# Fixing ScalarE's order around the token-major projections, folding a sigmoid into an eviction, and moving convolution taps to the sample part

## The chip, the cores and the metric

The kernel runs on one core of a Trainium2 chip. The metric is the time of one execution on the device, in microseconds. Beside that time the profile gives the span of one profiled execution, and the two are kept apart below.

## What is computed

One inference step of a decoder trunk with two layers. In each layer the rows of a prompt (16 learned tokens and 1024 new ones) and of 64 sample tokens (8 sequences of 8) are normalised and projected, and three mixers work on the projections: a gated linear recurrence, a depthwise convolution behind a gated linear unit (GLU), and sparse attention whose keys an indexer chooses. Their outputs are gated, merged, projected and added to the stream. Cut to what the change touches:

```python
def project(h, norm_g, w_in, b_in):
    u = rmsnorm(h, norm_g) @ w_in + b_in

def conformer_conv(glu_in, z, buf, conv_w, conv_b, ln_g, ln_b, conv_pw, w_pb):
    a, g = jnp.split(glu_in, 2, axis=-1)
    u = a * jax.nn.sigmoid(g)
    xp = jnp.concatenate([buf.astype(u.dtype), u], axis=1)
    y = lax.conv_general_dilated(xp, conv_w...) + conv_b       # 31 taps per channel, 512 channels

def index_scores(qi, wi, ki):
    s = jnp.einsum('bqhd,bsd->bqhs', qi.astype(F32), ki.astype(F32))
    return jnp.einsum('bqhs,bqh->bqs', jax.nn.relu(s), wi.astype(F32) * IDX_SCALE)
```

The keys of the indexer (`ki`), its queries (`qi`), the attention's keys and values pass through a rotation (rope) first. The scores of the prompt are computed against the 1040 prompt keys, those of the sample tokens against the cached pages and the 64 new keys; the best 256 keys of each query are then selected.

## The kernel before

Activations stand feature-major: 128 features on the partitions, 1104 tokens along the free axis, split into a high and a low part (`XH`, `XL`), and each weight likewise (`wh`, `wl`), so that a product takes three matmuls on TensorE (PE).

**Feature-major projections.** `stream` (L342 to L406) walks over chunks of 128 output features. A chunk has three token groups (384, 384 and 336 wide), each a chain of 24 matmuls into one PSUM bank, and ScalarE (ACT) evicts each group with its bias through the helper `act_` (L204), to a buffer `sp` that goes to DRAM after the third (L404): `gaD` and `ggD` are the value and the gate of the GLU, four chunks each. ACT casts the high part of the next weights (`wh<-wr`, L269), and GpSimd (POOL) subtracts for the low part (`wl`, L270). The stream is a generator: other stages call `fill(key)`, which issues so many matmuls' worth of it by a table.

**Token-major projections.** `cproj` (L658 to L693) computes what is needed token by token: keys, values, indexer queries and keys. Two groups of 290 columns, each nine token tiles of 24 matmuls (L679 to L681) into the banks that `stream` uses too (five banks in all); ACT evicts each tile to `CTr` (L684), POOL adds the bias (L685), and for the second column group VectorE (DVE) applies the rope (L718 to L722).

**Index keys and scores.** `indexer` (L725 on) casts the index keys (`rl<-CTr`, ACT L733), subtracts for the low part (POOL L734), transposes on PE (L739) and evicts to `KIH` and `KIL` (ACT L743, L744). Between these steps `fill` issues stream matmuls. L777 is the first PE step behind the last cast of a key. Then, for each tile of 128 queries and each of four heads, PE writes scores to one buffer of two banks (`lg`, L770, L771), ACT applies the relu (`rl<-lg`, L204) and DVE accumulates (L803, L805): the score loop. The sample part follows: POOL gathers pages of cached keys (`kir`, L880), PE transposes them (L888), ACT casts them, PE multiplies, and DVE builds the score rows in two rounds (L831, L833, L834); L869 writes the score bank anew.

**The taps.** `conv` (L1462 to L1503) has four chunks of 31 taps. A tap is two DVE operations, `cy<-up` on 128x1040 (L1495) and `cy<-us` on 128x64 (L1496); the first of a chunk is L1492 and L1493. `gated(c)`, called in the middle of the chunk before, loads the value into `up` and the gate into `cy` (L1473), applies the sigmoid in place on ACT (L1476), and multiplies on POOL (L1477, L1478, behind a memset L1470 and a copy L1475). `up` and `cy` have two buffers, so chunk 2 waits for chunk 0's last tap. Each tap costs 1420 units of a budget that the table `SIDE` gives to stages; a stage issues taps until its debt is paid: `t0` beside the feature-major chunks, `tr` (one value per token tile) behind each rope, `tk` behind the index keys, `ti` in the score loop, `ts` (twice per layer, once in each round) in the sample part. `SIDE` thus sets how many of a layer's 124 taps stand where in DVE's order.

**What sets the order.** PE's instructions stand in text order throughout, and DVE's from the attention stage on. Those of ACT, POOL and SyncE (SP) are placed by the scheduler of the framework, which estimates when each can start; on the chip every engine runs its list strictly in that order, and an instruction whose input is late holds up all behind it.

Of the kernel before, what the change touches and what calls it, by code (L numbers as in the profile page):

```python
# [11 lines left out]
def _quiet(msg, *args, **kwargs):  # L12
# [10 lines left out]
AF = mybir.ActivationFunctionType  # L23
# [26 lines left out]
SIDE = {"t0": (5000, 10000, 10000, 10000, 9300, 10000), "tr": (4200, 4200, 4200, 4200, 4200, 4200, 4200, 2000, 0),  # L50
# [3 lines left out]
KSEL = 4  # L54
# [100 lines left out]
def trunk(tc, a, o, depth=DEPTH):  # L155
# [47 lines left out]
    def act_(out, in_, fn, **kw):  # L203
        S.activation(out, in_, fn, **kw)  # L204
# [136 lines left out]
    def stream(l, pv, chunks, groups, slot, early, lead, more):  # L341


        n = len(chunks)
        blocks = chunks + [("early", (c, bi)) for c in range(8) for bi in range(2)]
        parts = [(c, g) for g in range(3) for c in range(lead)]
        parts += [(i, g) for i in range(lead, n - 2) for g in range(3)]
        parts += [(i, g) for g in range(3) for i in (n - 2, n - 1)]
        parts += [(i, g) for i in range(n, n + 16) for g in range(3)]
        ws, bufs = {}, {}  # L350

        def get(i):
            if i < len(blocks) and i not in ws:
                nm, c = blocks[i]
                if nm == "early":
                    ws[i] = ws[i - 2][1:] if c[0] % 2 else wpair(l, BLK["pb" if c[1] else "pa"] + c[0] // 2)
                else:
                    ws[i] = wchunk(l, BLK[nm] + c, V if i == lead else G, more if 1 < i < lead else None)

        get(0)  # L360
        get(1)
        yield True
        for i, g in parts:
            if g == 0 and 0 < i < lead - 1:
                get(i + 1)
            if lead <= i < n - 1 or i >= n or (i in (lead - 1, n - 1) and g == 2):
                get(i + 1)
            nm, c = blocks[i]
            if nm == "early":
                yield from early.part(c[1], c[0], g, ws[i][0], slot[0])  # L370
                continue
            bcol = BCOL[nm]
            wh, wl = ws[i]
            if g == 0:
                bufs[i] = spt(more if 1 < i < lead else None)
            n0, nn = groups(nm)[g]
            ps = slot[0]()[:, 0:nn]
            sl = slice(n0, n0 + nn)
            H, L = ([x[:, k, sl] for k in range(8)] for x in (XH, XL))
            if i == 0:  # L380

                ops = []
                for k in range(10):
                    if k < 8:
                        ops += [(wh(k), H[k]), (wl(k), H[k])]
                    if k > 1:
                        ops.append((wh(k - 2), L[k - 2]))
            else:
                ops = [(wh(k), x[k]) for k in range(8) for x in (H, L)] + [(wl(k), H[k]) for k in range(8)]
            for j, (w, x) in enumerate(ops):  # L390
                T.matmul(ps, w, x, start=(j == 0), stop=(j == 23))  # L391
                if j == 23:

                    fn = AF.Sigmoid if nm == "gate" and c < 16 else AF.Identity
                    act_(bufs[i][:, sl], ps, fn, bias=pv[:, bcol + c:bcol + c + 1])
                    if nm in ("cz",):

                        if g == 0:
                            sg = spt()
                        act_(sg[:, sl], ps, AF.Sigmoid, bias=pv[:, bcol + c:bcol + c + 1])  # L400
                        G.tensor_tensor(bufs[i][:, sl], bufs[i][:, sl], sg[:, sl], op=OP.mult)
                    if g == 2:
                        lo = groups(nm)[0][0]
                        S.dma_start(fD[nm][c, :, lo:NT], bufs[i][:, lo:NT])  # L404
                    if i == n - 1:
                        early.load(g)  # L406
                if j % 3 == 2:
                    yield True
# [164 lines left out]
    def layer(l, hst, late):  # L573
# [39 lines left out]
        slot[0] = mmt  # L613
        ctp = ctr.enter_context(tc.tile_pool(name="ctr", bufs=1, side="right"))
        CTr = ctp.tile([128, 9, 580], F32, name="CTr", tag="CTr")
        cproj(l, CTr, taps)
        scp = scs.enter_context(tc.tile_pool(name="scp", bufs=1))
        SC = scp.tile([128, SCN], F32, name="SC", tag="SC")
        SC8 = scp.tile([128, NT], F32, name="SC8", tag="SC8")
        fill("ic")  # L620
        indexer(l, CTr, SC, SC8, fill, taps)
        ctr.close()
        tk1 = tks.enter_context(tc.tile_pool(name="tk1", bufs=1))
        steps, F = topk(SC, SC8, tk1)
# [30 lines left out]
        return merge(l, pv, late_groups, fill, ers)  # L655


    def cproj(l, CTr, taps):  # L658
        with tc.tile_pool(name="cpk", bufs=CPK, side="right") as cpk, tc.tile_pool(name="cpr", bufs=2, side="right") as cpr, \
                tc.tile_pool(name="cpt", bufs=2, side="right") as cpt:  # L660
            for gi, (c0, w) in enumerate(CGROUPS):
                brep = cpr.tile([128, 290], F32, name="brep", tag="brep")
                Y.dma_start(brep[:, 0:w], a["b_in"][l, c0:c0 + w].partition_broadcast(128))
                ch, cl = [], []
                for k2 in range(4):
                    cr = cpr.tile([128, 2, 290], F32, name="cr", tag="cr")
                    Y.dma_start(cr[:, :, 0:w], a["wc"][l, gi, k2])
                    for k in range(2):
                        h_ = cpk.tile([128, 290], F32R, name="ch", tag="ch")
                        l_ = cpk.tile([128, 290], F32R, name="cl", tag="cl")  # L670
                        S.copy(h_[:, 0:w], cr[:, k, 0:w])
                        G.tensor_tensor(l_[:, 0:w], cr[:, k, 0:w], f(h_[:, 0:w]), op=OP.subtract)
                        ch.append(h_)
                        cl.append(l_)
                for t in range(9):
                    rows, ts = TROWS[t], slice(128 * t, 128 * t + TROWS[t])
                    ps = dmt()
                    for k in range(8):
                        T.matmul(ps[0:rows, 0:w], XH[:, k, ts], ch[k][:, 0:w], start=(k == 0), stop=False)  # L679
                        T.matmul(ps[0:rows, 0:w], XH[:, k, ts], cl[k][:, 0:w], start=False, stop=False)  # L680
                        T.matmul(ps[0:rows, 0:w], XL[:, k, ts], ch[k][:, 0:w], start=False, stop=(k == 7))  # L681
                    d0 = c0 - O_C - 512
                    dst = CTr[0:rows, t, d0:d0 + w]
                    S.copy(dst, ps[0:rows, 0:w])  # L684
                    G.tensor_tensor(dst, dst, brep[0:rows, 0:w], op=OP.add)  # L685
                    if gi == 1:
                        rope(CTr[0:rows, t, 0:576].rearrange("p (h d) -> p h d", d=64), 9, t, rows, cpt, ((0, 2), (4, 9)))
                        taps("tr", t)
            for dst, j0, j1 in ((kvD.rearrange("t p c -> (t p) c"), 0, 256), (o["kv"][l], 0, 256), (o["ki"][l], 512, 576)):
                Y.dma_start(dst[0:1024].rearrange("(t p) c -> p t c", p=128), CTr[:, 0:8, j0:j1])  # L690
                Y.dma_start(dst[1024:NT], CTr[0:80, 8, j0:j1])
# [30 lines left out]
            V.tensor_tensor(x[:, h0:h1, 0:16], A[0:rows, h0:h1], B[0:rows, h0:h1], op=OP.add)  # L722


    def indexer(l, CTr, SC, SC8, fill, taps):  # L725
        with tc.tile_pool(name="ixc", bufs=1) as xc, tc.tile_pool(name="ixt", bufs=2) as xt:
            KIH = xc.tile([128, NT], F32R, name="KIH", tag="KIH")
            KIL = xc.tile([128, NT], F32R, name="KIL", tag="KIL")
# [6 lines left out]
            for t0 in range(0, 9, 4):  # L735
                n = min(4, 9 - t0)
                ps, w = tpt(), 0
                for t in range(t0, t0 + n):
                    T.transpose(ps[:, w:w + TROWS[t]], kk[0:TROWS[t], t], ident[0:TROWS[t], 0:TROWS[t]])  # L739
                    w += TROWS[t]  # L740
                sl = slice(128 * t0, 128 * t0 + w)
                for e in (slice(0, 64), slice(64, 128)):
                    S.copy(KIH[e, sl], ps[0:64, 0:w])  # L743
                    S.copy(KIL[e, sl], ps[64:128, 0:w])  # L744
                if t0 == 8:
                    V.tensor_tensor(ki8, f(KIH[0:64, sl]), f(KIL[0:64, sl]), op=OP.add)
                fill("ik", t0 // 4)

            wsc = xc.tile([128, 9, 4], F32, name="wsc", tag="wsc")
            V.tensor_scalar(wsc[:, 0:8], CTr[:, 0:8, 576:580], 0.0625, None, op0=OP.mult)  # L750
# [713 lines left out]
    def conv(l, pv, cw, c1):  # L1464
        def gated(c):
# [7 lines left out]
            Y.dma_start(y, fD["gg"][c])  # L1473
            Y.dma_start(sr[:, 0], a["state_conv"][l, c])
            G.tensor_copy(us[:, :, 0:30], sr[:, 0])  # L1475
            act_(y, y, AF.Sigmoid)  # L1476
            G.tensor_tensor(up[:, 30:1070], up[:, 30:1070], y[:, 0:1040], op=OP.mult)  # L1477
            G.tensor_tensor(us[:, :, 30:38], us[:, :, 30:38], y[:, 1040:1104].rearrange("p (b q) -> p b q", q=8), op=OP.mult)  # L1478

# [6 lines left out]
        for c in range(4):  # L1486
            up, us, y = nxt
# [288 lines left out]
```

## Time and profile before

| | |
|---|---|
| median of 3 runs | 2927.29 us (2923.65 to 2928.7) |
| profiled execution, time | 2926.8 us |
| profiled execution, span | 2924.9 us |
| mean granted clock of TensorE | 0.979 |
| busy: PE, DVE, ACT, POOL | 94%, 72%, 41%, 43% of the span |

The span covers the first to the last instruction; 1.9 us lie around it. A row of a timeline gives the start, the duration and, in brackets, how long the engine had idled and what ended the wait. Time is saved where PE idles, since it is busy for 94% of the span; idle time of the other engines matters where PE waits for them. The two layers run the same program; layer 0's stage of interest lies at 100 to 460 us, layer 1's at 1540 to 1860 us.

### The profile page before, as it was taken

How to read it: one execution, taken by the hardware profiler on the slowest of the kernel's cores; microseconds unless marked ns; L12 is line 12 of the kernel's file. 1: busy time of each engine (PE TensorE's matmuls, PEld its weight loads, DVE VectorE, ACT ScalarE, POOL GpSimd, SP SyncE). 2: the span in 40 equal slices, each digit the busy share in tenths (PEclk: the TensorE clock that was granted, in tenths of full speed). 3: DMA queues.
4: the chain of work that ended last, by engine and by line, in shares of the span. 5: the costliest groups of instructions: out<-in, count | busy, mean ns of one | idle time of the engine just before them, and what ended most of it. 6: DMA issues, size and time to landing. Idle time of an engine off the chain costs nothing. (4 is left out here: it accounts for less than half of the span.)

```text
span 2924.9 us, 44993 instructions
## 1 busy us (share of the span) xinstructions
PE 2757.9 (94%) x17094; PEld 2620.9 (90%) x17094; DVE 2113.7 (72%) x3832; ACT 1186.8 (41%) x2369; POOL 1247.6 (43%) x978
## 2 busy tenths in 40 slices
PE   7989899999998999999999998998999999999898
PEld 7988879999998888879999997898999989988798
DVE  5798867889969667535366896788899786774443
ACT  4314443323333556544341334422332335565432
POOL 3533334434425214756564332443434241157563
PEclk9999999999999999999999999999999999999999
DMA  4523234332335124666453322323332441247554
GB/s 146 162 61 109 90 103 140 122 112 89 118 130 170 67 67 154 195 201 197 150 169 105 98 83 90 127 99 109 130 112 77 157 151 63 86 150 222 190 166 148
DMA packets 192569, 374.14 MB, mean 128 GB/s; under 512 B 30657, under 2 KB 129697, under 8 KB 192289
## 3 DMA queue, kind: packets, MB, share of 16 engines
q1 hardware_dynamic: 166016, 272.21, 29.7%
q10 hardware_dynamic: 20448, 78.09, 6.6%
q0 software_dynamic: 5888, 20.97, 2.3%
q8 instruction: 134, 2.20, 0.3%
q14 instruction: 83, 0.67, 0.1%
HBM read 251.07 MB, written 122.40 MB: 128 GB/s over the span
## 5 line engine op out<-in xcount | busy, mean ns | idle before, releaser
L391 PE MATMUL mm<-xh,wh 128*128 128x384 f32 (+2 forms) x2656 | 888.1, 336 | 27.6 <-ACT sp L204 23.9
L391 PE MATMUL mm<-xl,wh 128*128 128x384 f32 (+2 forms) x2656 | 886.0, 336 | 0.0
L270 POOL TENSOR_TENSOR wl<-wr,wh 128x512 fp32r<-128x512 f32 x332 | 473.1, 1443 | 697.8 <-ACT wh L269 465.8
L391 PEld LDWEIGHTS mm<-xh,wh 128*128 128x128 f32 x2656 | 506.0, 191 | 41.5 <-ACT sp L204 29.0
L391 PE MATMUL mm<-xh,wl 128*128 128x384 f32 (+2 forms) x2656 | 531.3, 336 | 0.0
L391 PEld LDWEIGHTS mm<-xl,wh 128*128 128x128 f32 x2656 | 506.2, 191 | 7.2 <-issue 1.9
L391 PEld LDWEIGHTS mm<-xh,wl 128*128 128x128 f32 x2656 | 461.8, 192 | 6.3 <-issue 1.9
L916 DVE TENSOR_SCALAR_CACHE_REDUCE jk<-SC,F 80x1104 bf16<-80x1104 f32 (+6 forms) x448 | 448.8, 1002 | 8.4
L204 ACT ACTIVATE sp<-mm,vec 128x384 f32<-128x384 f32 (+1 forms) x356 | 198.6, 564 | 512.0 <-PE mm L391 494.8
L1495 DVE SCALAR_TENSOR_TENSOR cy<-up,vec,cy 128x1040 f32<-128x1040 f32 x240 | 337.9, 1408 | 0.4
L269 ACT CAST wh<-wr 128x512 fp32r<-128x512 f32 x352 | 203.6, 618 | 164.1 <-PE mm L391 80.4
L204 ACT ACTIVATE P<-P,nm 128x896 f32<-128x896 f32 (+7 forms) x128 | 99.5, 778 | 64.1 <-DVE nm L1021 61.7
L1037 DVE TENSOR_TENSOR pl<-tp,ph 128x512 fp32r<-128x512 f32 x144 | 97.8, 687 | 36.9 <-ACT ph L1036 36.1
L1496 DVE SCALAR_TENSOR_TENSOR cy<-us,vec,cy 128x64 f32<-128x64 f32 x240 | 117.2, 488 | 0.0
L1036 ACT CAST ph<-tp 128x512 fp32r<-128x512 f32 x144 | 83.2, 584 | 54.4 <-PE tp L1033 50.2
L1021 DVE CUSTOM_DVE_ANT_0 P<-sc,MB 128x512 f32<-128x512 f32 (+1 forms) x96 | 63.9, 667 | 57.1 <-PE sc L1015 56.2
L1346 PEld LDWEIGHTS lg<-hQ,hK 128*128 128x128 f32 x512 | 65.8, 205 | 28.0 <-issue 19.9
L1025 DVE TENSOR_SCALAR P<-P,nm 128x896 f32<-128x896 f32 (+7 forms) x128 | 87.4, 683 | 4.3
L1346 PE MATMUL lg<-hQ,hK 128*128 128x64 f32 x512 | 66.4, 286 | 25.5 <-DVE hQ L1375 25.3
L1033 PE MATMUL tp<-ident,P 128*128 128x128 f32 x576 | 88.0, 275 | 1.5 <-DVE P L1025 1.5
L204 ACT ACTIVATE rl<-lg 128x1024 f32<-128x1024 f32 (+6 forms) x54 | 42.6, 788 | 102.8 <-DVE SC L805 60.2
L287 PE MATMUL tp<-xh,wh 128*128 128x384 f32 (+2 forms) x240 | 79.9, 335 | 0.4 <-DVE z L1681 0.4
(454 smaller groups left out, 5932.0 us busy)
## 6 DMA issues: line engine op xcount, KB each, us to landing
wr<-in_wp SPq DMA_DIRECT2D x180, 512.0 KB
eg<-gateD SPq DMA_DIRECT2D x80, 184.0 KB
gateD<-sp ACTq DMA_DIRECT2D x24, 552.0 KB
gateD<-sp ACTq DMA_DIRECT2D x24, 544.0 KB
cr<-in_wc SPq DMA_DIRECT2D x16, 290.0 KB
gt<-gateD SPq DMA_DIRECT2D x24, 192.0 KB
za<-zaD SPq DMA_DIRECT2D x24, 192.0 KB
ggD<-sp ACTq DMA_DIRECT2D x8, 552.0 KB
```

The costliest lines, as they stand in the source:

```text
L204: S.activation(out, in_, fn, **kw)
L269: S.copy(wh[:, k:k + 4], wr[:, k:k + 4])
L270: (eng or G).tensor_tensor(wl[:, k:k + 4], wr[:, k:k + 4], f(wh[:, k:k + 4]), op=OP.subtract)
L391: T.matmul(ps, w, x, start=(j == 0), stop=(j == 23))
L916: V.tensor_scalar(jk[0:rows, 0:n], s, F.bitcast(F32)[0:rows, j:j + 1], None, op0=OP.is_ge, op1=OP.add, accum_out=cnt[0:rows, j:j + 1])
L1025: V.tensor_scalar(p[:, 0:n], p[:, 0:n], nm[:, 3:4], None, op0=OP.mult)
L1033: T.transpose(ps[:, 128 * c:128 * c + 128], P[c][:, 128 * kt:128 * kt + 128], ident)
L1036: S.copy(ph, ps)
L1037: V.tensor_tensor(pl, ps, f(ph), op=OP.subtract)
L1346: T.matmul(ps[:, 64 * c:64 * c + 64], K[:, 128 * c:128 * c + 128], up(Q[:, 128 * c:128 * c + 128], m), start=True, stop=True)
L1495: V.scalar_tensor_tensor(yp, up[:, j:j + 1040], w, yp, op0=OP.mult, op1=OP.add)
L1496: V.scalar_tensor_tensor(ys, us[:, :, j:j + 8], w, ys, op0=OP.mult, op1=OP.add)
```

## The change

Three things change. `SIDE`: the budgets of `tr` and `ti` fall and that of `ts` rises. By the debts, a layer's 124 taps stand 39, 22, 3, 43 and 17 in `t0`, `tr`, `tk`, `ti` and `ts` before, and 39, 12, 3, 38 and 32 after. The gate chunks 2 and 3 get their sigmoid in `stream`'s eviction, and `conv` applies it only for chunks 0 and 1. In `cproj` the casts and subtractions of both column groups stand ahead of both groups' matmuls, and from the first eviction to the last cast of the index keys ACT's order is that of the text.

```diff
-SIDE = {"t0": (5000, 10000, 10000, 10000, 9300, 10000), "tr": (4200, 4200, 4200, 4200, 4200, 4200, 4200, 2000, 0),
-        "tk": 4200, "ti": (1400, 2800, 2800, 2800, 2800, 2800), "ts": 3000,
+SIDE = {"t0": (5000, 10000, 10000, 10000, 9300, 10000), "tr": (2400, 2400, 2400, 2400, 2400, 2400, 2400, 600, 0),
+        "tk": 4200, "ti": (1400, 2400, 2400, 2400, 2400, 2400), "ts": 5800,
...
-                    fn = AF.Sigmoid if nm == "gate" and c < 16 else AF.Identity
+                    fn = AF.Sigmoid if (nm == "gate" and c < 16) or (nm == "gg" and c >= 2) else AF.Identity
...
-        cproj(l, CTr, taps)
+        act = ExitStack()
+        cproj(l, CTr, taps, act)
...
-        indexer(l, CTr, SC, SC8, fill, taps)
+        indexer(l, CTr, SC, SC8, fill, taps, act)
...
-    def cproj(l, CTr, taps):
+    def cproj(l, CTr, taps, act):
...
+            groups = []
             for gi, (c0, w) in enumerate(CGROUPS):
...
+                groups.append((gi, c0, w, brep, ch, cl))
+
+            act.enter_context(tc.manual_schedule(engines={mybir.EngineType.Activation}))
+            for gi, c0, w, brep, ch, cl in groups:
                 for t in range(9):
...
-    def indexer(l, CTr, SC, SC8, fill, taps):
+    def indexer(l, CTr, SC, SC8, fill, taps, act):
...
                 fill("ik", t0 // 4)
+            act.close()
...
-            act_(y, y, AF.Sigmoid)
+            if c < 2:
+                act_(y, y, AF.Sigmoid)
```

PE's order does not change, and behind the sample part no engine's does. The first place is ACT's list in layer 0 at the token-major evictions (`CTr<-` is an eviction, `cy<-cy` the sigmoid of chunk 2, `sp` an eviction of the stream). Before:

```order
L684 COPY CTr<-tp 128x290
L684 COPY CTr<-mm 128x290 x2
L684 COPY CTr<-tp 128x290 x2
L204 ACTIVATE cy<-cy 128x1104
L684 COPY CTr<-tp 128x290
L684 COPY CTr<-mm 128x290 x2
L684 COPY CTr<-tp 80x290
```

Now (line numbers grow by six here, as the diff adds lines):

```order
L404 DMA gaD<-sp 128x1104
L690 COPY CTr<-tp 128x290
L690 COPY CTr<-mm 128x290 x2
L690 COPY CTr<-tp 128x290 x3
L690 COPY CTr<-mm 128x290 x2
L690 COPY CTr<-tp 80x290
```

The sigmoid between the fifth and the sixth eviction is gone. In layer 1 the one of chunk 2 stood ahead of the last three `sp` evictions before the first `CTr`, and is gone too.

The second place is ACT's list right behind the last of the 18 evictions (`rl<-CTr` is the cast of the index keys, `wh<-wr` a cast of the stream's next weights). Before:

```order
L684 COPY CTr<-mm 80x290
L204 ACTIVATE sp<-mm,vec 128x384 x2
L733 CAST rl<-CTr 128x8x64
L269 CAST wh<-wr 128x512 x2
L204 ACTIVATE sp<-mm,vec 128x336
L404 DMA vD<-sp 128x1104
L733 CAST rl<-CTr 80x64
L204 ACTIVATE sp<-mm,vec 128x384
```

Now:

```order
L690 COPY CTr<-mm 80x290
L269 CAST wh<-wr 128x512 x2
L204 ACTIVATE sp<-mm,vec 128x384 x2
L204 ACTIVATE sp<-mm,vec 128x336
L404 DMA vD<-sp 128x1104
L269 CAST wh<-wr 128x512 x2
L204 ACTIVATE sp<-mm,vec 128x384
L739 CAST rl<-CTr 128x8x64
L739 CAST rl<-CTr 80x64
```

Both casts of the index keys now stand behind four `sp` evictions, not the first behind two.

The third place is POOL's list in layer 0 beside the evictions (`CTr<-CTr,brep` adds the bias, `up<-up,cy` is the GLU's product of chunk 2). Before:

```order
L685 TENSOR_TENSOR CTr<-CTr,brep 128x290 x2
L1470 MEMSET up 128x30
L1475 COPY us<-sr 128x8x30
L685 TENSOR_TENSOR CTr<-CTr,brep 128x290 x3
L1477 TENSOR_TENSOR up<-up,cy 128x1040
```

Now:

```order
L691 TENSOR_TENSOR CTr<-CTr,brep 128x290 x2
L1477 MEMSET up 128x30
L1482 COPY us<-sr 128x8x30
L691 TENSOR_TENSOR CTr<-CTr,brep 128x290 x2
L1485 TENSOR_TENSOR up<-up,cy 128x1040
L691 TENSOR_TENSOR CTr<-CTr,brep 128x290
```

The product still stands among the bias adds, now between the fourth and the fifth, and waits for the load of the gate rather than for ACT.

## Rows read from the trace of the kernel before

**Rows 1.** First part of the page: engine, busy us (share of the span), instructions.

```profile
PE 2757.9 (94%) x17094; PEld 2620.9 (90%) x17094; DVE 2113.7 (72%) x3832; ACT 1186.8 (41%) x2369; POOL 1247.6 (43%) x978
```

**Rows 2.** Waits of PE, layer 0, 100 to 460 us: total us, times, longest us.

```profile
PE mm L391 <- ACT sp L204: 7.4, 3, 4.3
PE tp L679 <- ACT CTr L684: 6.2, 1, 6.2
PE lg L770 <- ACT rl L204: 4.1, 4, 1.6
```

**Rows 3.** Waits of PE, layer 1, 1540 to 1860 us (the row of rows 2 for L770 stands here too).

```profile
PE mm L391 <- ACT sp L204: 3.6, 3, 1.7
PE mm L679 <- ACT sp L204: 3.2, 1, 3.2
...
PE tp L777 <- ACT KIL L744: 2.0, 1, 2.0
PE tp L739 <- POOL rl L734: 1.0, 1, 1.0
```

**Rows 4.** Timeline of ACT, layer 0: start, us, engine, line, [idle before <-releaser].

```profile
144.21 0.40 ACT L684 COPY CTr<-tp 128x290 f32<-128x290 f32 x1 [2.83 <-PE tp L681]
165.09 1.12 ACT L204 ACTIVATE cy<-cy 128x1104 f32<-128x1104 f32 x1 [20.48 <-DMA cy<-ggD]
...
194.69 0.40 ACT L684 COPY CTr<-mm 80x290 f32<-80x290 f32 x1 [2.83 <-PE mm L681]
```

**Rows 5.** Windows: stretch, PE busy us (instructions), PEclk, DMA share, GB/s.

```profile
166.00:168.00 2.00, 1.44 (x6) 0.50 0.00 0
```

**Rows 6.** Timeline of PE, layer 0, index keys.

```profile
215.18 0.54 PE L391 MATMUL mm<-xh,wh 128*128 128x384 f32 x1 [4.29 <-ACT sp L204]
...
219.48 0.34 PE L391 MATMUL mm<-xh,wh 128*128 128x384 f32 x1
...
226.21 0.79 PE L777 MATMUL tp<-wsc,cb 80*128 80x4 f32 x6 [1.69 <-ACT KIL L744]
```

**Rows 7.** Timeline of ACT, layer 0, index keys.

```profile
213.03 0.62 ACT L733 CAST rl<-CTr 128x512 fp32r<-128x512 f32 x1 [9.39 <-DVE CTr L722]
```

**Rows 8.** Timeline of DVE, layer 0: first and last rope of the token-major part.

```profile
174.06 0.79 DVE L718 TENSOR_TENSOR rA<-CTr,cb 128x144 f32<-128x144 f32 x1 [3.68 <-POOL CTr L685]
...
219.37 0.34 DVE L722 TENSOR_TENSOR CTr<-rA,rB 80x32 f32<-80x32 f32 x2
```

**Rows 9.** Windows of the score loop: busy us (x) of PE, PEld, DVE, ACT, POOL.

```profile
250.00:300.00 50.00, 46.16 (x270) 44.09 (x268) 49.77 (x62) 19.00 (x33) 15.26 (x10) 1.00 0.16 55
```

**Rows 10.** Timeline of DVE, layer 0, sample part.

```profile
337.31 1.30 DVE L1495 SCALAR_TENSOR_TENSOR cy<-up,vec,cy 128x1040 f32<-128x1040 f32 x1
...
345.77 1.30 DVE L1495 SCALAR_TENSOR_TENSOR cy<-up,vec,cy 128x1040 f32<-128x1040 f32 x1
346.98 1.32 DVE L1496 SCALAR_TENSOR_TENSOR cy<-us,vec,cy 128x64 f32<-128x64 f32 x1
348.22 2.35 DVE L1495 SCALAR_TENSOR_TENSOR cy<-up,vec,cy 128x1040 f32<-128x1040 f32 x1
...
367.23 0.23 DVE L831 TENSOR_TENSOR SC<-ac,cb 80x80 f32<-80x80 f32 x1 [15.05 <-PE ac L828]
...
390.96 1.22 DVE L833 TENSOR_TENSOR SC<-SC,lg 80x1024 f32<-80x1024 f32 x1 [11.82 <-PE lg L828]
```

**Rows 11.** Timeline of POOL, layer 0.

```profile
166.29 2.40 POOL L1477 TENSOR_TENSOR up<-up,cy 128x1040 f32<-128x1040 f32 x1 [6.22 <-ACT cy L204]
...
346.51 2.96 POOL L270 TENSOR_TENSOR wl<-wr,wh 128x512 fp32r<-128x512 f32 x2
...
384.73 2.49 POOL L270 TENSOR_TENSOR wl<-wr,wh 128x512 fp32r<-128x512 f32 x2 [16.75 <-ACT wh L269]
```

**Rows 12.** Timeline of PE, sample part, first matmul that reuses the score bank.

```profile
392.95 0.40 PE L869 MATMUL lg<-KIH,qt 128*64 128x512 f32 x1
```

## The prediction

> **What bounds the kernel now.** The page's first part comes first: PE is busy for 2757.9 of 2924.9 us [rows 1], so 167 us of idle PE are all that an edit which leaves PE's work alone can take. The waits of PE in the changed stretch say whose they are. In layer 0, 6.2 us are one wait of the token-major matmuls for their eviction, 7.4 us are three waits of the stream for `sp` evictions (the longest 4.3), and 4.1 us are four waits of the score matmuls for the relu [rows 2]. In layer 1 the row of the score matmuls reads word for word the same; the others are smaller, 3.2 and 3.6, with 2.0 and 1.0 at the index keys [rows 3]. All name ACT, which is busy 41% of the time, so it isn't ACT's speed; its timeline shows the head of its list waiting while ready evictions stand behind it.
>
> Two places show this. Between the fifth and the sixth token-major eviction stands the sigmoid of chunk 2: it idles 20.48 us for the load of the gate and starts at 165.09 [rows 4]. That load could not start earlier, as its buffer is chunk 0's, which DVE is still using. PE has filled all five banks by then and stops. Its clock falls as well: 0.50 was granted from 166 to 168 us, right behind the idle time [rows 5]. The second place is the cast of the index keys: 9.39 us idle for the last ropes [rows 7], with an `sp` eviction behind it for which PE waits 4.29 us [rows 6]. The ropes are late because DVE issues 22 taps between the first, which starts at 174.06, and the last, which ends near 219.7 [rows 8]. In the score loop DVE itself is the slow one, 49.77 of 50 us busy against PE's 46.16 [rows 9]: relu buffers come free late, ACT waits for them, PE for ACT.
>
> **The change part by part.** The sum is against the profiled execution, 2926.8 us, half a microsecond under the median.
>
> *Sigmoid out of the evictions, layer 0.* Evictions paced by PE follow each other by 0.40 + 2.83 = 3.23 us [rows 4]. From the fifth at 144.21 the eighteenth would come at 144.21 + 13 x 3.233 = 186.2, and it comes at 194.69. That is 8.45 us: 6.2 of waiting and 2.2 at half clock. The sigmoid inside the stream's eviction replaces one activation by another of the same shape; four separate ones of 1.12 us go [rows 4]. **8.4 us.**
>
> *The same in layer 1.* There the sigmoid stands ahead of three `sp` evictions, and PE waits 3.2 us [rows 3]; with the clock behind it at the proportion of layer 0 but a shorter gap, I take 0.4. **3.6 us.**
>
> *The index keys, layer 0.* With ten taps fewer at 1.41 us alone (six taps from 337.31 to 345.77 [rows 10]) and about 1.6 with POOL beside them (an estimate: 45.6 us from the first rope to the last, less nine ropes, over 22), the last rope ends some 16 us sooner, near 203.5. Its start doesn't move much: the first rope waits for a bias add that stands behind the GLU product on POOL, and that product, at 166.29 behind the sigmoid [rows 11], still waits for the same load. PE would finish the 35 stream steps after the projections at about 186.0 + 17.9 = 203.9 (35 steps of three matmuls, 368 columns in the mean, at the token-major rate of 3.233 us for 24 matmuls of 290 columns). So the waits of 4.29 and 1.69 us go, and some 1.3 us of low clock behind the first (0.54 us a matmul against 0.34 [rows 6]). One wait is new: both casts now stand behind four evictions, so cast (0.62 [rows 7]) and POOL's subtraction (about 1.5) begin only when PE has done its 35 steps, and the transposes wait. Bounds: nothing, if ACT comes earlier than I think, and 4 us, if the ropes or the two `wl` subtractions ahead on POOL (2.96 us for two [rows 11]) hold it up; I take 2.0. 4.29 + 1.69 + 1.3 - 2.0 = **5.3 us.**
>
> *The index keys, layer 1.* 2.0 and 1.0 us [rows 3] and the first of the `sp` waits, 0.4, less the same 2.0: **1.4 us.**
>
> *Score loop.* Five taps fewer are 8 us of DVE in some 100. The four waits sum to 4.1 us a layer; DVE then has spare time and I leave 0.5: **3.6 us twice.** The `sp` wait at the end of the loop, 1.7 in both layers (the longest of layer 1's three [rows 3]), has ACT standing behind a DVE product: **1.4 us twice.** The sigmoid of chunk 3 also leaves the loop; ACT had idle time there, so nothing.
>
> *Sample part.* Fifteen taps more, 16 in each of two rounds. Round one: from 337.31 to the row that waits for PE at 367.23 there are 29.9 us [rows 10]; 16 taps take 22.5, and two `wl` subtractions cost 1.04 + 1.06 (a small tap 1.32 instead of 0.28, a large one 2.35 instead of 1.29 beside them, at 346.98 and 348.22 [rows 10, 11]): 24.7, covered. Round two: from 367.4 to 390.96 there are 23.6 us; 16 taps and the `wl` pair at 384.73 [rows 10, 11] take 22.5 + 2.1, and 0.4 for the end of an earlier pair: 25.0. L833 then ends at 393.6, and the matmul that overwrites its scores, at 392.95 [rows 12], waits 0.6. Bounds: 0 if the pair falls outside, 2.2 if a second pair is met; **-0.6 us twice.**
>
> By the Trainium skill (SBUF — State Buffer, "Who interferes with whom") a DVE instruction with two SBUF inputs, as a tap has, and a GpSimd instruction that reads SBUF exclude each other for a whole instruction. By that rule a `wl` pair can cost round two its whole 2.96 us, PE would wait 1.5 us instead of 0.6, and the time would be 2902. The trace shows the exclusion at 346.98 and 348.22, but 2.1 us of it, so I keep the row.
>
> *Casts of both groups first.* They are hidden: PE does stream chunks there without a wait. If the casts came late, PE's first token-major matmul would wait.
>
> Sum: 8.4 + 3.6 + 5.3 + 1.4 + 7.2 + 2.8 - 1.2 = 27.5 us, so 2926.8 - 27.5 = 2899.3, and 2900 with the half microsecond of the median.
>
> **The rivals.** *Only the sigmoid's stall goes.* ACT in text order waits for the ropes just as before, only with other work behind it. For it: POOL's product still holds the bias adds until 166 or so, and my margin of the ropes is under a microsecond. If they end 4 us later than I think, the index keys gain 1 in layer 0 and lose in layer 1; if the score loop gives half, the sum is 12.0 + 0 + 3.6 + 2.8 - 1.2 = 17, or 2910. Against it: ten taps are over 14 us of a DVE that idles at no point of that stretch.
>
> *The gain is given back.* The taps only changed place, and DVE may become the bound behind them: 30 taps now run where DVE had idled 15.05 and 11.82 us for PE [rows 10]. If the selection that follows starts no earlier than before, the time is 2927 less a few, say 2925. Against it: both idle times end on PE, so DVE's start moves with PE's.
>
> *The sample part turns slower.* If the taps there meet POOL's subtractions and gathers throughout, every second one costs 1.32 + 2.35 = 3.67 us and the mean is 2.54. Round one then takes 40.6 for 29.9 us of room, round two 40.6 for 23.6: 27.7 us a layer, 55 in all, against 28.7 gained elsewhere: +27, or 2954. It decides from a mean tap of 2.12 us, where 16 x (2.12 - 1.87) + 16 x (2.12 - 1.47) are the 14.4 gained per layer. Against it: POOL has three `wl` pairs in that stretch, and six taps beside the gathers ran at 1.41.
>
> **How the numbers follow.** My forecast has a chance of 0.70, the first rival 0.18, giving back 0.07, slower 0.05. The forecast's own range comes from its bounds: no new waits (+4), no score waits (+1) and a free sample part (+1.2) give 2894; the new waits at 4 each (-4), the sample part at 2.2 (-3.2) and half the score loop (-3.6) give 2911. I take 2890 to 2917, which holds the first rival too and leaves out the last two, 0.12, and tails. A measurement tells 0.2%, 5.9 us, from no change: faster by more is 0.70 + 0.18 = 0.88, within it 0.07, slower 0.05.
>
> **What would show it.** In the changed profile token-major evictions at a pace of 3.23 us from the first to the eighteenth; no granted clock of 0.50 there; the cast of the index keys behind the fourth eviction with no idle time on a rope; a wait of PE for POOL's subtraction of 1 to 3 us at the transposes; score waits under 1 us a layer; 16 taps of 1.4 us in each round with L833 less than 2 us behind PE. I am wrong if the cast idles for a rope, if taps in the sample part average over 1.9 us, or if the waits behind it grow by what was gained ahead.

## The result, and the profile after

The changed kernel takes 2893.27 us (median of 4, 2886.44 to 2899.35) against 2927.99 for the kernel before (4 runs, 2923.65 to 2931.37): a ratio of 0.9882, 95% interval 0.9866 to 0.9899. Two more sets on other occasions gave 0.9896 (0.9881 to 0.9911) and 0.9902 (0.9888 to 0.9916). Medians and ratios are of executions in the fast state; two of those below were in a slow one. The forecast was 2900, range 2890 to 2917. The profiled execution, the slowest of the four, took 2899.35 us: 27.45 less than the profiled one before, where the sum said 27.5; by the medians of the three sets the gain is 29 to 35 us. That the single terms were worth what the sum gave them is another matter; the experiments say no.

The first part of the page and the waits of PE in both layers (to set beside [rows 1 to 3]; line numbers are six to eight higher behind the edit):

```profile
PE 2751.2 (95%) x17094; PEld 2614.6 (90%) x17094; DVE 2120.3 (73%) x3832; ACT 1183.9 (41%) x2365; POOL 1249.3 (43%) x978
```

Layer 0, 100 to 460 us:

```profile
PE mm L391 <- ACT sp L204: 3.8, 3, 1.5
...
PE tp L745 <- POOL rl L740: 2.8, 1, 2.8
...
PE lg L876 <- DVE SC L840: 0.6, 1, 0.6
PE tp L784 <- ACT KIL L750: 0.3, 1, 0.3
```

Layer 1, 1500 to 1860 us:

```profile
PE tp L745 <- POOL rl L740: 1.0, 1, 1.0
PE lg L876 <- DVE SC L840: 0.8, 1, 0.8
```

The token-major wait of 6.2 us, layer 1's 3.2 and the score matmuls' 4.1 in each layer have no row any more. Two kinds are new in layer 0, and both were forecast: the transposes wait for POOL's subtraction (in layer 1 they waited 1.0 us before too), and the matmul that overwrites the scores waits for the second round's score row. ACT's timeline in layer 0 has the first and the last eviction, then the two casts of the index keys:

```profile
129.36 0.40 ACT L690 COPY CTr<-tp 128x290 f32<-128x290 f32 x1 [2.69 <-PE tp L687]
...
184.32 0.40 ACT L690 COPY CTr<-mm 80x290 f32<-80x290 f32 x1 [2.83 <-PE mm L687]
...
202.84 0.62 ACT L739 CAST rl<-CTr 128x512 fp32r<-128x512 f32 x1 [1.71 <-DVE CTr L728]
204.99 0.25 ACT L739 CAST rl<-CTr 80x64 fp32r<-80x64 f32 x1 [1.53 <-DVE CTr L728]
```

The eighteen evictions are 3.233 us apart, and the granted clock beside them is full (stretch, PE busy, PEclk, DMA share, GB/s):

```profile
156.00:166.00 10.00, 10.00 (x76) 1.00 0.22 62
```

DVE's timeline holds the last step of a rope that took 3.73 us beside POOL's gather, add and subtractions (0.34 for most others), the last rope, and the second round of the sample part:

```profile
185.81 3.73 DVE L728 TENSOR_TENSOR CTr<-rA,rB 128x32 f32<-128x32 f32 x2
...
203.48 1.42 DVE L728 TENSOR_TENSOR CTr<-rA,rB 80x32 f32<-80x32 f32 x2
...
347.51 0.24 DVE L838 TENSOR_TENSOR SC<-ac,cb 80x80 f32<-80x80 f32 x1 [9.07 <-PE ac L835]
...
372.69 1.21 DVE L840 TENSOR_TENSOR SC<-SC,lg 80x1024 f32<-80x1024 f32 x1
```

From L838 to L840 it is 25.2 us (25.0 was forecast), and L840, which waited 11.82 us for PE before [rows 10], now waits for nothing. Where the 27.45 us came, read off the stores of the stream, which are the same 120 in both traces:

| stretch | forecast | measured |
|---|---|---|
| ahead of the change (first stores, at 69 us) | 0 | 1.9 |
| layer 0 to the last token-major eviction | 8.4 | 8.45 |
| from there to the first PE step behind the key casts | 5.3 | 4.5 |
| layer 1, both | 5.0 | 6.0 |
| score loop with the eviction at its end, layer 0 and 1 | 5.0 and 5.0 | 6.9 and 6.6 |
| sample part, layer 0 and 1 | -0.6 and -0.6 | -2.8 and -2.2 |
| behind it, both layers | 0 | -1.9 |

In all three profiled executions of the changed kernel the stretches of the change sum to 27.4, 26.8 and 24.9 us, so what the medians gain beyond that lies elsewhere. Of the stretches, the one from the last eviction to the first step behind the key casts differs most: 4.5, 4.9 and 2.0.

### The profile page after: what moved, and what is told of

It reads as the page before. It is cut to its first block, busy times and chain, and to the rows that moved or that the text cites. A ratio compares the mean times of both kernels' runs of the same rounds, so it can differ in the third digit from the quotient of the medians.

```text
span 2897.4 us, 44994 instructions
## 1 busy us (share of the span) xinstructions
PE 2751.2 (95%) x17094; PEld 2614.6 (90%) x17094; DVE 2120.3 (73%) x3832; ACT 1183.9 (41%) x2365; POOL 1249.3 (43%) x978
## 5 line engine op out<-in xcount | busy, mean ns | idle before, releaser
L391 PE MATMUL mm<-xh,wh 128*128 128x384 f32 (+2 forms) x2656 | 887.9, 336 | 22.5 <-ACT sp L204 19.1
L391 PE MATMUL mm<-xl,wh 128*128 128x384 f32 (+2 forms) x2656 | 884.0, 335 | 0.0
L270 POOL TENSOR_TENSOR wl<-wr,wh 128x512 fp32r<-128x512 f32 x332 | 481.2, 1467 | 714.7 <-ACT wh L269 452.3
L391 PEld LDWEIGHTS mm<-xh,wh 128*128 128x128 f32 x2656 | 505.9, 190 | 36.8 <-ACT sp L204 24.5
L391 PE MATMUL mm<-xh,wl 128*128 128x384 f32 (+2 forms) x2656 | 530.4, 336 | 0.0
L391 PEld LDWEIGHTS mm<-xl,wh 128*128 128x128 f32 x2656 | 505.5, 190 | 7.1 <-issue 1.7
L391 PEld LDWEIGHTS mm<-xh,wl 128*128 128x128 f32 x2656 | 460.2, 191 | 6.2 <-issue 1.7
L269 ACT CAST wh<-wr 128x512 fp32r<-128x512 f32 x352 | 203.5, 618 | 157.8 <-PE mm L391 76.6
```

The lines of the kernel that those rows point to most:

```text
L269: S.copy(wh[:, k:k + 4], wr[:, k:k + 4])
L270: (eng or G).tensor_tensor(wl[:, k:k + 4], wr[:, k:k + 4], f(wh[:, k:k + 4]), op=OP.subtract)
```

## The experiments

**The rival theories.** The prediction adds its terms as if each edit had its own price (the sum theory). The rope theory says that up to the index keys one chain sets the end: gate load, GLU product, bias adds, ropes with taps between them, key casts. A stall ahead of a late rope then costs nothing, and ACT's order pays only where the ropes are early. All eight combinations of the three edits separate them.

**The sigmoid alone.**

```diff
-                    fn = AF.Sigmoid if nm == "gate" and c < 16 else AF.Identity
+                    fn = AF.Sigmoid if (nm == "gate" and c < 16) or (nm == "gg" and c >= 2) else AF.Identity
...
-            act_(y, y, AF.Sigmoid)
+            if c < 2:
+                act_(y, y, AF.Sigmoid)
```

> The kernel before with the sigmoid of gate chunks 2 and 3 in the eviction, nothing else. Sum theory (each term of the prediction is worth its own amount, whatever the other parts do): token-major evictions without a stall, 8.4 us sooner in layer 0 and 3.6 in layer 1 and kept, so 12 us faster. Rope theory (up to the index keys the end is set by DVE's chain gate load, GLU product on POOL, bias adds, ropes with 22 taps between them, so the eviction stall was hidden behind it): the eighteenth eviction comes 8.4 us sooner in layer 0, but the last rope stays within 2 us of 219.7, PE waits in the stream or at the transposes instead, and the first PE step behind the last key cast (226.2 before) moves by under 2 us; in layer 1 the ropes themselves start 3.6 us sooner. 3 to 6 us faster in all.

Measured: 0.9972 (0.9963 to 0.9980). Rows of PE, then of ACT, in layer 0:

```profile
214.43 0.69 PE L391 MATMUL mm<-xh,wh 128*128 128x384 f32 x1 [13.37 <-ACT sp L204]
...
225.47 0.79 PE L777 MATMUL tp<-wsc,cb 80*128 80x4 f32 x6 [1.53 <-ACT KIL L744]
```

```profile
184.87 0.40 ACT L684 COPY CTr<-mm 80x290 f32<-80x290 f32 x1 [2.83 <-PE mm L681]
...
212.28 0.62 ACT L733 CAST rl<-CTr 128x512 fp32r<-128x512 f32 x1 [18.46 <-DVE CTr L722]
```

The evictions end 9.8 us sooner than at 194.69 [rows 4], 1.4 of it from an earlier start, and ACT idles 9.1 us more for the rope: 18.46 instead of 9.39 [rows 7]. PE waits 13.37 us in one piece instead of 6.2 and 4.3, and L777 stands where it stood, 226.21 [rows 6]. In layer 0 the sigmoid in the eviction is worth nothing alone; in layer 1 the ropes start with the evictions and 3.5 us are kept. The total, 8 us, is some 5 better than that and beyond the 3 to 6 of the rope theory (interval 6 to 11); the last section comes to it.

**The taps alone.**

```diff
-... "tr": (4200, 4200, 4200, 4200, 4200, 4200, 4200, 2000, 0),
+... "tr": (2400, 2400, 2400, 2400, 2400, 2400, 2400, 600, 0),
-... "ti": (1400, 2800, 2800, 2800, 2800, 2800), "ts": 3000,
+... "ti": (1400, 2400, 2400, 2400, 2400, 2400), "ts": 5800,
```

> The kernel before with the new SIDE table alone; the scheduler then places both casts of the index keys on ACT right behind the eighteenth eviction, ahead of two evictions of the stream. Sum theory: the sigmoid's stall stays, the index keys, the score loop and the sample part give 5.3 + 1.4 + 10.0 - 1.2 = 15.5 us. Rope theory: the last rope ends near 203.5 instead of 219.7 although the stall is there (eighteenth eviction still at 194.7), PE waits about 2 us for the evictions behind the casts, and the first PE step behind the key casts comes 11 to 12 us sooner in layer 0 and 4 to 5 in layer 1; with the score loop some 25 us in all, nearly the whole change.

Measured: 0.9959 (0.9946 to 0.9972), 12 us. The last rope does come near 201 with the stall in place, and the waits of the score matmuls for the relu vanish. But the step behind the key casts comes only 7 us sooner, not 11: my expectation forgot the 6 us that PE's own work takes between its 35th stream step and that row. The 18 us from the last eviction are now PE's, and the stall stands in front of them:

```profile
165.65 0.61 PE L679 MATMUL tp<-ch,xh 128*128 128x290 f32 x1 [4.86 <-ACT CTr L684]
...
219.61 0.79 PE L777 MATMUL tp<-wsc,cb 80*128 80x4 f32 x6 [0.34 <-ACT KIL L744]
```

Of the 25 us that I expected in all, 12 came: layer 1 up to the key casts gave 1.7 instead of 4 to 5, and the two sample parts took 6.3.

**Sigmoid and order, taps as before.**

> The change with SIDE as it was before: sigmoid in the eviction and ACT in text order, taps in their old places. Sum theory: 12 us faster, as the sigmoid's terms don't need the taps. Rope theory: no stall of the evictions, but the last rope stays near 219, both casts of the keys stand behind it and behind four evictions, PE idles some 15 us at the transposes, and the first step behind the key casts comes at 226 to 229 us, no sooner than before; layer 1 gains about 2. Within 5 us of the kernel before, of either sign.

Measured: 0.9973 (0.9963 to 0.9983). PE and ACT in layer 0:

```profile
217.38 1.97 PE L745 MATMUL tp<-ident,rl 128*128 128x128 f32 x8 [12.79 <-POOL rl L740]
```

```profile
215.08 0.62 ACT L739 CAST rl<-CTr 128x512 fp32r<-128x512 f32 x1 [11.43 <-DVE CTr L728]
219.79 0.25 ACT L739 CAST rl<-CTr 80x64 fp32r<-80x64 f32 x1 [4.08 <-DVE CTr L728]
```

The 8.4 us of stall are gone and 12.79 us of waiting stand at the transposes. The sum theory's 12 us are outside the interval (5 to 11), and the rope theory's "within 5" is at its edge, though its rows came: layer 0 stands still, layer 1 gains 1.5 up to the key casts, and most of what else the profiled pair gains is the wait in the last section.

**Order alone.**

> The kernel before with ACT's text order alone; the sigmoid of chunk 2 then stands behind the thirteenth eviction, when its data have landed, and POOL's product behind twelve bias adds. If the order is what removes the eviction stall and the sigmoid in the eviction adds nothing, this is the run with order and sigmoid over again: no wait of a token-major matmul, the last rope near 219, PE idle some 13 us at the transposes, and the same time within 3 us, 8 us faster than before. If the sigmoid in the eviction is worth its stall, it is as slow as before.

Measured: 0.9986 (0.9977 to 0.9995). Text order does remove the stall by itself, since the sigmoid then stands behind the twelfth eviction (I had said the thirteenth); PE waits 13.04 us at the transposes of layer 0, as in the run with the sigmoid:

```profile
217.27 1.97 PE L745 MATMUL tp<-ident,rl 128*128 128x128 f32 x8 [13.04 <-POOL rl L740]
```

In layer 1, where POOL's product now stands among the bias adds, PE waits 6.0 us at the transposes instead of 3.6, and nothing is gained. This run is some 4 us behind the other, and layer 1 shows 2.4 of them: half right.

**Taps and sigmoid, ACT's order left to the scheduler.**

> The change without ACT's text order: taps moved and sigmoid in the eviction, the casts of the second column group and ACT's order left to the scheduler, which puts both casts of the index keys right behind the eighteenth eviction, ahead of the stream's. Sum theory (the order is worth nothing by itself): as fast as the changed kernel, within 3 us. Rope theory: evictions without a stall, but the casts then hold ACT until the last rope near 203, two stream evictions wait behind them, PE idles some 9 us in the stream in layer 0 with a low clock after it, and the first step behind the key casts comes at 219 to 222 instead of 211; layer 1, whose ropes come sooner than PE, as in the changed kernel. 7 to 11 us slower than the changed kernel, some 20 faster than before.

Measured: 0.9933 (0.9921 to 0.9946), 9 to 10 us slower than the changed kernel, as the rope theory said. With the casts of the keys right behind the last eviction, ACT waits for the rope and PE for ACT:

```profile
205.73 0.65 PE L391 MATMUL mm<-xh,wh 128*128 128x336 f32 x1 [10.44 <-ACT sp L204]
```

**Taps and order, the sigmoid left in `conv`.**

> The change with the sigmoid of chunk 2 and 3 left in conv. In text order it stands behind the fifteenth token-major eviction, when its data have long landed. Sum theory: the stall is gone all the same, so as fast as the changed kernel, within 3 us. Rope theory: the GLU product on POOL now waits until about 178, the bias adds stand behind it, the first rope comes near 182 instead of 170 and the last near 212, and PE idles some 10 us at the transposes of layer 0, about 7 in layer 1. 12 to 17 us slower than the changed kernel.

Measured: 0.9910 (0.9896 to 0.9924), as fast as the changed kernel within the intervals; my rope-theory figure of 12 to 17 us was wrong. ACT, then PE:

```profile
173.64 0.40 ACT L690 COPY CTr<-tp 128x290 f32<-128x290 f32 x1 [2.83 <-PE tp L687]
173.94 1.13 ACT L204 ACTIVATE cy<-cy 128x1104 f32<-128x1104 f32 x1
```

```profile
205.30 1.09 PE L745 MATMUL tp<-ident,rl 128*128 128x128 f32 x8 [0.96 <-POOL rl L740]
```

The sigmoid waits for nothing behind the fourteenth eviction (I had said the fifteenth). I had left POOL's product where it was; the scheduler moved it behind fourteen bias adds, so the first rope comes at 168.8 against 169.67 in the changed kernel, whose run had started 2.3 us sooner, and PE waits 0.96 us instead of 2.78. Beside the order, the edit of the sigmoid is thus worth nothing that these runs can tell.

The eight together; for layer 0 the times of three rows, each less the run's own offset at the store of the second value chunk (80.09 us before), and for layer 1 the distance from the last gate store to the step behind the key casts ("last rope" is the start of its last row):

| taps | order | sigmoid | ratio | 18th eviction | last rope | step behind key casts | layer 1 |
|---|---|---|---|---|---|---|---|
| old | old | old | 1 | 194.7 | 219.4 | 226.2 | 100.9 |
| old | old | new | 0.9972 | 186.2 | 220.0 | 226.8 | 97.5 |
| old | text | old | 0.9986 | 186.2 | 219.0 | 225.6 | 101.8 |
| old | text | new | 0.9973 | 186.2 | 218.8 | 225.5 | 99.4 |
| new | old | old | 0.9959 | 192.7 | 200.9 | 219.2 | 99.2 |
| new | old | new | 0.9933 | 186.2 | 202.7 | 222.9 | 93.8 |
| new | text | old | 0.9910 | 186.2 | 202.7 | 211.5 | 95.0 |
| new | text | new | 0.9896 | 186.2 | 205.4 | 213.3 | 95.0 |

With the taps in their old places the step behind the key casts never comes before 225 in layer 0, whatever is done to ACT. With them moved, order is worth 8 to 10 us there, and the sigmoid nothing or less. Order is one edit here, but it does two things: it removes the stall and puts the key casts behind the stream's evictions. In the run without order the sigmoid's edit had removed the stall and the step still came at 222.9, so what order adds there, 9.6 us, comes from the place of the casts (the 10.44 above); the casts moved with the stall left standing were not run. Most rows came as the rope theory said, its totals mostly did not.

**The same kernel again.**

> The changed kernel as it is, for its distance from the others on one chip. Both theories: 27 to 35 us faster than before (the profiled pair differs by 27.5, the medians by 34.7). If the gain is the profiled pair's, the interval lies around 0.9906; if the medians' is nearer, around 0.988.

> The changed kernel beside these on the same chip: 0.988 to 0.991 of before.

Measured: 0.9896 and 0.9902. The first two profiled spans agree, 2897.4 and 2898.2; the third was 2892.5.

**More taps in the sample part.**

```diff
-        "tk": 4200, "ti": (1400, 2400, 2400, 2400, 2400, 2400), "ts": 5800,
+        "tk": 4200, "ti": (1400, 1840, 1840, 1840, 1840, 1840), "ts": 7200,
```

> The changed kernel with 20 taps instead of 16 in each round of the sample part and eight fewer in the score loop (ts 7200, ti 1400 and five of 1840). If the second round's room of 23.6 us is what I measured, the four taps more there come straight to PE: its wait for the score row grows from 0.6 and 0.8 to about 6.2 us in each layer, with a spell of low clock behind it, the first round still fits, the score loop loses under 2 us of waits; 8 to 14 us slower than the changed kernel. If DVE had spare time there (rival: the wait is hidden by later work), within 3 us of it.

Measured: 0.9943 (0.9930 to 0.9956), 10 to 14 us slower than the changed kernel. PE, both layers:

```profile
376.85 0.69 PE L876 MATMUL lg<-KIH,qt 128*64 128x512 f32 x1 [6.19 <-DVE SC L840]
...
1806.84 0.69 PE L876 MATMUL lg<-KIH,qt 128*64 128x512 f32 x1 [6.72 <-DVE SC L840]
```

6.2 was expected. The second round is at its edge with 16 taps, and a tap more costs its 1.4 us at once.

**The taps of the sample part split unevenly.** First with two taps taken from the ropes:

```diff
-... "tr": (2400, 2400, 2400, 2400, 2400, 2400, 2400, 600, 0),
+... "tr": (2400, 2400, 2400, 2400, 2400, 1200, 1200, 0, 0),
-... "ts": 5800,
+... "ts": (7750, 4600),
...
-                    taps("ts")
+                    taps("ts", g)
```

> The changed kernel with ts of 7750 in the first round (21 taps) and 4600 in the second (13), and two taps fewer behind the last ropes. PE's waits of 0.6 and 0.8 us for the score row go, the wait of 2.8 at the transposes of layer 0 falls to 1 to 1.5; 2 to 4 us faster than the changed kernel, at the edge of what can be told. If the first round's 29.9 us hold no 21 taps, PE waits for L838 and it is slower.

Measured: 0.9905 (0.9890 to 0.9919), no gain. The two waits fell as expected (0.96 at the transposes, none for the score row), but score waits came back (1.28 in layer 0) and PE waited longer for the first gather: 4.77 us against 3.25 in the changed kernel. PE, POOL and DVE there:

```profile
326.06 1.09 PE L895 MATMUL tp<-ident,kir 128*128 128x128 f32 x4 [4.77 <-DMA kir<-in_cache_kidx,rowid]
```

```profile
321.13 1.45 POOL L887 DMA_INDIRECT kir<-in_cache_kidx,rowid  x1 [4.80 <-PE tp L895]
322.89 1.90 POOL L887 DMA_INDIRECT kir<-in_cache_kidx,rowid  x1 [0.30 <-issue]
```

```profile
321.65 0.81 DVE L1500 TENSOR_SCALAR cy<-up,vec 128x1040 f32<-128x1040 f32 x1
```

In the changed kernel these two gathers took 1.03 and 0.95 us, and the first tap of chunk 3, L1500, ran two us before them; here it runs beside the first. So the next run moves only the split:

```diff
-... "ts": 5800,
+... "ts": (7250, 4350),
```

> The changed kernel with 20 taps in the first round of the sample part and 12 in the second, nothing else; the first tap of chunk 3, the operation with one input, stays where it is, two taps into the first round. Theory (it was that one operation beside a page gather that made the gather land late when it had moved there): gathers land in 3.6 to 3.9 us and PE waits for them as in the changed kernel, 3.2 to 3.5 us, and the waits for the score row, 0.6 and 0.8, go. 1 to 3 us faster than the changed kernel. Rival (more taps in the round starve the gathers): the waits for the first gather grow to 4.8 in both layers, no gain.

Measured: 0.9880 (0.9864 to 0.9895), beside 0.9902 for the changed kernel in the same set. The score row waits are gone in both layers, and the first gather costs what it did, with 20 taps in that round:

```profile
325.89 0.81 PE L895 MATMUL tp<-ident,kir 128*128 128x128 f32 x4 [3.48 <-DMA kir<-in_cache_kidx,rowid]
```

That tells the number of taps apart from their kind. The run with more taps points at L1500 too: there it runs beside the third gather of both layers, and the fourth takes 1.91 us in both, as the second did above. But L1500 was not moved by itself, and before the change, with two-input taps alone beside it, a first gather took 1.42 us and PE waited 3.63, so the cause is not shown.

**Both small terms.** The split, and the sigmoid in `conv`.

> The same split, and the sigmoid back in conv, where ACT's text order puts it behind the fifteenth eviction and POOL's product behind the bias adds. If both small terms are real and independent, the wait at the transposes of layer 0 falls from 2.8 to 1.0 and the score row waits go: 3 to 5 us faster than the changed kernel, the fastest of all. If not, as fast as it within 2 us.

Measured: 2888.7 us, 0.9872 (0.9856 to 0.9888), the lowest median of all and 7 us under the changed kernel beside it; the two intervals touch at 0.9888. The score row waits are gone, but the wait at the transposes of layer 0 was 2.16 us this time, not 1.0, and the stretches of the change sum to 27.9 us, against 27.4, 26.8 and 24.9 in the changed kernel. By these profiles at most 3 of the 7 us lie there, and that the two terms add up is not shown.

## Why the prediction was right, and where not

The time, the direction and the views were right: ACT at 41% held PE up by the order of its list, and the trace after has the evictions at 3.23 us without a break, no low clock there, no score waits, and the new waits where they were expected. That the sum met the profiled pair to 0.05 us is luck: stretches that gave 3.5 (score loop) and 1.0 (layer 1) more than forecast stand against 3.8 (sample part) and 0.8 (index keys) less, and 1.9 us ahead of the change against 1.9 behind it. The sizes:

- *The stall of layer 0, 8.4 us.* The stretch gave 8.45. But "sigmoid out of the evictions" as the cause, with its own price, failed: the sigmoid's edit gives nothing there in any of the four comparisons, text order removes the stall too, and neither shortens layer 0 while the ropes are late. The term belongs to taps and order together. My own sentence that the ropes were late should have told me that a stall ahead of them was hidden. Nor was it DVE alone that held the gate's load back: chunk 0's last tap ended at 155.8 in the trace before, and the load, issued at 161.39, waited its last 3.3 us for the store of that chunk's result (`yD<-cy`).
- *The index keys, 5.3 and 1.4 us.* 4.5 in layer 0; with 3.6 for the stall, 6.0 in layer 1 against 5.0. The new wait, taken as 2.0, was 2.78 and 0.96. In layer 0 the cast idled for a rope (1.71 and 1.53 us), which I said would show me wrong: the last rope ended at 204.9 in a run that stood 1.9 us ahead, so 3.3 us later than the 203.5 I gave it. The first rope, which I said would hardly move, even came 2.5 us sooner, so the ropes and their taps took 5.8 us more than I gave them; 3.4 of these are the one step that stood beside POOL's work for 3.73 us.
- *The score loop, 5.0 with its eviction.* 6.9 and 6.6. In layer 0 the rows of waits hold 5.4 of it (4.1 for the relu, 1.7 for the eviction and 0.7 for a query before, 1.1 for the eviction after); the rest I did not trace. The wait for the eviction, which I let fall by 1.4, fell by 0.6 and 0.9.
- *The sample part, -0.6.* The wait itself was 0.59 and 0.84, and 25.2 us for the round against 25.0. Not foreseen was a wait of the stream, 1.24 and 1.23 us, for an eviction that stands behind ACT's casts of the sample queries (L391 in both layers). The stretches lost 2.8 and 2.2.
- *The first rival, 2910.* Its mechanism is real, late ropes with ACT in text order, and its condition nearly came: the last rope was 3.3, 2.9 and 3.8 us late in the three executions. The index keys of layer 0 then gave 4.5, 4.9 and 2.0 where it had 1 for 4 us, and layer 1 lost nothing. Its 12 us for the stall don't stand alone either: with the taps in their old places sigmoid and order give 8 in all.
- *Giving back* did not come: behind the sample parts the two layers lose only 1.9 us together.
- *The slower rival* did not come: taps ran at 1.41 us beside the gathers. Its edge was near, though: four taps more per round give back a third of the gain or more.
- *The shared port.* The Trainium skill's rule (SBUF — State Buffer, "Who interferes with whom") would have made the second round's pair of subtractions cost 2.96 us and the time 2902. The two operations beside that pair took 1.29 and 2.35 us after the change, 2.1 more than alone as before, and the round agreed with the rows. The rope's step of 3.73 us went the other way: it took 3.4 more than elsewhere, about the length of an add and two subtractions on POOL (0.71 and 2.54 us), and ended 0.2 us behind them. So neither price holds everywhere.

```profile
186.14 0.71 POOL L691 TENSOR_TENSOR CTr<-CTr,brep 80x290 f32<-80x290 f32 x1
186.80 2.54 POOL L270 TENSOR_TENSOR wl<-wr,wh 128x512 fp32r<-128x512 f32 x2
```

## What to carry to other kernels

Before a stall is given a price, look at what the next step waits for: a gap of 8 us ahead of a rope that is 16 us late is worth nothing. Once the ropes are early, text order, which closes the gap and moves the casts, is worth 8 to 10 us, but closing the gap without moving the casts was still worth nothing in layer 0. So test edits that touch one chain in all combinations, not one by one. An in-order engine's list should be written so that a cast waiting for a slow producer stands behind everything that is ready, and work moved to idle stretches should be counted against the room up to the row that waits for PE: 23.6 us held 16 taps, with 0.6 to 0.8 us of waiting, and not 20.

## What the runs showed of the hardware

The same wait at the same place costs different amounts of clock. PE waited 3.25 us for the gather in two executions of the changed kernel. Granted clock behind it (fourth column), the first execution, then the second:

```profile
322.00:324.00 2.00, 1.25 (x8) 0.84 0.14 25
324.00:326.00 2.00, 2.00 (x9) 0.50 0.36 115
326.00:328.00 2.00, 2.00 (x11) 0.80 0.58 204
```

```profile
320.00:322.00 2.00, 0.00 (x0) 0.87 0.42 123
322.00:324.00 2.00, 1.09 (x4) 0.50 0.44 139
324.00:326.00 2.00, 1.88 (x8) 0.50 0.00 0
326.00:328.00 2.00, 2.00 (x9) 0.50 0.55 141
328.00:330.00 2.00, 2.00 (x13) 0.93 0.80 286
```

The clock missing is 2 x (0.16 + 0.50 + 0.20) = 1.7 us in the one and 2 x (0.13 + 3 x 0.50 + 0.07) = 3.4 in the other. In time they differ by less, since part of the low clock of the second fell into the wait itself. From the end of the wait to the same later row PE took 9.69 us in the first (from 321.27), 0.84 of it a wait for the next gather, and 9.93 in the second (from 322.76), 0.28 of it such a wait, so without these they are 0.8 us apart:

```profile
330.96 1.91 PE L861 MATMUL lg<-kib,qs 64*32 64x512 f32 x8
```

```profile
332.69 1.91 PE L861 MATMUL lg<-kib,qs 64*32 64x512 f32 x8
```

In the third execution it took 9.05 with 0.40 of waiting, behind a wait of 3.39 us. Runs of one kernel spread over 14 us (the kernel before: 2917.95 to 2932.1 in 23); whether such differences add up to that is not shown. Another that comes and goes is a wait far behind the change, at a step of the recurrence: 2.19 us in the profile before, with low clock from 774 to 782, and 0.69 without it in the run with the sigmoid alone, where the stretch is 4.6 us shorter. It is 2.19 in the first two profiles of the changed kernel and 1.02 in the third, so it belongs to no edit. In the profiled pair it is most of what the sigmoid alone gained beyond its 3.5 us; that twelve runs of that kernel lie 8 us under before, and why the wait comes and goes, stays open.
